# Waits by VectorE's counted work, wide products among the inverse's small ones, alternating score heads and earlier loads of the plain pair, in one layer of a hybrid trunk

## The chip, the cores and the metric

The kernel runs on one core of one Trainium2 chip. The metric is the device time of one execution in microseconds. Before the change it is 2060.8 us, the median of three runs (2058.53 to 2061.56).

## The reference

One layer on x of 1024 tokens x 1024 channels, f32: a half-weighted SwiGLU block (ffn1, width 2816), four token mixers in parallel with an output product, a second SwiGLU block (ffn2) and a final norm.

```python
def swiglu_ffn(x, w_in, w_out):
    gate, up = jnp.split(x @ w_in, 2, axis=-1)
    return (jax.nn.silu(gate) * up) @ w_out
...
    y = jnp.concatenate([y_pool, y_hgrn, y_rwkv, y_gla], axis=-1).astype(u.dtype)
    return y @ w_out
...
        x = x + 0.5 * swiglu_ffn(rms_norm(x, norm_ffn1[l]), ffn1_w_in[l], ffn1_w_out[l])
        x = x + token_mixer(rms_norm(x, norm_mix[l]), w_in[l], w_out[l], ...)
        x = x + 0.5 * swiglu_ffn(rms_norm(x, norm_ffn2[l]), ffn2_w_in[l], ffn2_w_out[l])
    return rms_norm(x, norm_final)
```

Three of the mixers carry a state along the tokens: HGRN2 and GLA are chunked gated linear attention, and RWKV7 is the recurrence

```python
        s_kk = jnp.einsum('bhvk,bhk->bhv', S, kk_t)
        S = (S * w_t[:, :, None, :] - s_kk[..., None] * (kk_t * a_t)[:, :, None, :]
             + v_t[..., :, None] * k_t[:, :, None, :])
        return S, jnp.einsum('bhvk,bhk->bhv', S, r_t)
```

The fourth is a moving average over 2 to 16 tokens. Each mixer has 256 of the 1024 channels (four heads of 64).

## The kernel before

**Precision and products.** A wide f32 product is done as three products of 128x128 by 128x512 in float32r, from a high part (`whi`, `xs`) and a low part (`wlo`, the second half of `xs`): ScalarE casts the high part, VectorE subtracts it for the low part (`wload`, lines 145 and 146, for weights; `split`, lines 177 to 181, for activations). These are the dense products here. All PE instructions go through `te.matmul` (line 89) or `te.transpose` (line 96).

**Stages.** ffn1_in, ffn1_out, the mixers (`weave`), w_out, ffn2_in, ffn2_out and the final norm. The two FFN output stages work on pairs of 128-row tiles with seven products in place of eight (`out_seven`, lines 622 to 675); one pair, PLAIN, is left for the end and done plainly: in ffn1_out its four h tiles and four weights are loaded and split after `out_seven`, then 16 output tiles follow, each of six products, whose VectorE part adds to x (line 747) and splits the sum for the mixers (line 181).

**The weave.** The mixers are generators ("threads") that do a few instructions and yield the time after which their next step may run. RWKV is one thread: four units (two pairs of heads for each half of 512 tokens) one after another. A unit fetches its inputs, prepares them on ScalarE and VectorE (lines 1206 to 1280), forms the scores (lines 1285 to 1294), inverts 64x64 triangles (`inverse`, lines 1411 to 1490: out by DMA, 28 operations on GpSimd, back by DMA, then six steps of 32 or 16 small products on PE with copies between), runs eight chunks of three steps, and starts its group norm, which stores y. GLA and HGRN2 are another thread (`gates`, lines 1491 to 1600). Two threads `rstd_steps` (lines 219 to 235) form the norm of each half. The dense stream is one generator too: the projections `w_in` of half 0 and half 1, for half 0 w_out's products (`wout_early`, line 1723), which need all of that half's y, and corner products of ffn2_in. After the weave, `w_out` does the products of half 1, which need y of the fourth RWKV unit last (ORDER, line 1707), and ffn2_in follows.

**What sets the order.** `weave` (line 882) keeps a clock `te.clk`, to which each PE instruction adds a modelled time. It takes the thread with the earliest ready time that has come, and otherwise three dense products. A yielded number of `LAT` (line 34) is added to the clock for the thread's next ready time. When the dense stream has nothing to give, the clock jumps to the next ready time. The order of PE's instructions that comes out is fixed in the program; the other engines' order follows the priorities that the steps get. The clock that the planner keeps is a model and is not measured on the chip.

Of the kernel before, what the change touches and what calls it, by code (L numbers as in the profile page):

```python
# [16 lines left out]
P = 128  # L17
# [18 lines left out]
           pool=10.0, decay=2.9, rstd=3.0, rstd1=7.0, consts=14.4, rs0=2.8, rs1=4.2)  # L36
# [32 lines left out]
class PE:  # L69
# [15 lines left out]
    def matmul(self, out, lhsT, rhs, **kw):  # L85
        n = 1
        for d in out.shape[1:]:
            n *= d
        return self._add(self.nc.tensor.matmul(out, lhsT=lhsT, rhs=rhs, **kw),  # L89
                         n * 0.42e-3 if rhs.dtype == F32R else max(n * 1.68e-3, 0.04))  # L90

    def transpose(self, out, src, ident):
        n = 1
        for d in out.shape[1:]:
            n *= d
        return self._add(self.nc.tensor.transpose(out, src, ident), max(n * 0.85e-3, 0.03))

# [6 lines left out]
class Trunk:  # L104
    def __init__(self, tc, ctx, A, out):
        self.tc, self.nc, self.A, self.out = tc, tc.nc, A, out
# [11 lines left out]
        make_identity(nc, self.ident)  # L118
# [486 lines left out]
    def out_seven(self, wk, w_out, slot, tmp, blocks, early, acc, after=None):  # L605
# [36 lines left out]
        for i, (b0, nb) in enumerate(blocks):  # L642
# [5 lines left out]
            for q in range(4):  # L648
# [28 lines left out]
                for m, w in zip(self.ORDER7, weights(raw, nb)):  # L677
# [29 lines left out]
                    if last and q == 3 and after is not None:  # L707
                        after(m)
                raw = nraw
            hs = nhs  # L710

    def ffn1_out(self, wk, w_out):
# [17 lines left out]
        def h_tile(f, h):  # L730
# [3 lines left out]

        self.out_seven(wk, w_out, slot, lambda: wk.tile([P, H], F32, name="tmp"),
                       ((9, 2), (1, 2), (3, 2), (5, 2), (7, 2)), (8, 8, 8, 8, 0), acc)
        f0 = 2 * PLAIN
        hs = [[h_tile(f, h) for h in range(2)] for f in (f0, f0 + 1)]
        w = [self.wload([(wo[:, f0:f0 + 2, n * P:(n + 2) * P], 0, None)], 2, 256, 1) for n in range(0, KT, 2)]
# [10 lines left out]
    def ffn2_out(self, wk, w_out):  # L750
# [54 lines left out]
        self.out_seven(wk, w_out, slot, tmp, ((9, 2), (1, 2), (3, 2), (5, 2), (7, 2)), (12, 12, 12, 12, 0), load_acc,  # L805
                       after)
        gf = wk.tile([P, D], F32, name="wrawb", bufs=2)
        nc.scalar.dma_start(gf, self.A["norm_final"].broadcast_to([P, D]))
        self.gf = gf

        def h_tile(f, h):
            t = tmp()
            nc.sync.dma_start(t, self.hd[f, h])
            return self.split(t)

        hp = [[h_tile(f, h) for h in range(2)] for f in (f0, f0 + 1)]
# [65 lines left out]
    def weave(self):  # L882

        te = self.te
        te.on, te.last, te.clk = True, None, 0.0
        consts = self.mix_consts()
        next(consts)
        self.threads = [Thread(self.rstd_steps(0), LAT["rs0"]), Thread(self.rstd_steps(1), LAT["rs1"]), Thread(self.ysplit()), Thread(consts, LAT["consts"]), Thread(self.rwkv()), Thread(self.gates())]
        dense = self.dense_stream()
# [12 lines left out]
    def step(self, t):  # L902
        te, tc = self.te, self.tc
        p = tc.cur_priority
        tc.cur_priority = p - URGENT
        r = next(t.gen, self)
        tc.cur_priority += URGENT
# [304 lines left out]
    def rwkv_unit(self, pr, h):  # L1212
# [72 lines left out]
        for c2 in range(4):  # L1285
            ps = self.px.tile([P, 4, P], F32, name="px")
            hd = c2 // 2
            hs = slice(hd * 64, hd * 64 + 64)
            for i in range(4):
                c = 4 * (c2 % 2) + i  # L1290
                te.matmul(ps[:, i], lhsT=bk[hs, c].rearrange("p x t -> p (x t)"), rhs=rK[hs, c].rearrange("p x t -> p (x t)"), start=True, stop=True)
            ss = slice(4 * c2, 4 * c2 + 4)
            nc.vector.tensor_tensor(Ak[:, ss], ps[:, :, 64:128], mask(64), op=ALU.mult)
            nc.vector.tensor_tensor(Ar[:, ss], ps[:, :, 0:64], mask(0), op=ALU.mult)
            if c2 in (1, 2):
                yield LAT["score"]
# [116 lines left out]
    def inverse(self, Ak):  # L1413
# [30 lines left out]
        for b in range(2):  # L1444
# [3 lines left out]
            for s in range(16):  # L1448
                te.transpose(pv[:, s], XT[bs, s, bs], self.ident[bs, bs])
# [4 lines left out]
        for b in range(2):  # L1454
            bs, b2 = slice(b * 32, b * 32 + 16), slice(b * 32, b * 32 + 32)
            for s in range(16):
                te.matmul(pv[b2, s], lhsT=XT[bs, s, b2], rhs=Xn[bs, s], start=True, stop=True)
# [4 lines left out]
        for b in range(2):  # L1462
            bs, b2 = slice(b * 32, b * 32 + 16), slice(b * 32, b * 32 + 32)
            for s in range(16):
                te.matmul(pv[bs, s], lhsT=Y[b2, s], rhs=XT[b2, s, b * 32 + 16:b * 32 + 32],
                                 start=True, stop=True)
# [8 lines left out]
        for s in range(16):  # L1475
            te.transpose(ps[0:32, s], XT[0:32, s, 0:32], self.ident[0:32, 0:32])
# [3 lines left out]
        for s in range(16):  # L1480
            te.matmul(ps[32:64, s], lhsT=XT[0:32, s, 32:64], rhs=Xn[:, s], start=True, stop=True)
# [3 lines left out]
        for s in range(16):  # L1485
            te.matmul(ps[0:32, s], lhsT=Y[32:64, s], rhs=XT[32:64, s, 32:64], start=True, stop=True)
# [366 lines left out]
```

## Time and profile before

| what | value |
|---|---|
| median of three runs | 2060.8 us (2058.53 to 2061.56) |
| the profiled execution | 2059.14 us |
| its span in the trace | 2057.3 us |
| mean granted TensorE clock | 0.983 |
| DMA | 348.60 MB, 169 GB/s |

A row of the timeline has the start, the length and the engine of one instruction or of several alike in a row (x4), then its line, operation, output<-inputs and shapes; in brackets the idle time before it on its engine and what ended that. An f32 product counts as two records, a dense product as one. A row of the busy times by stretch has the stretch, its length, the busy time of each engine with its instructions, and then the granted clock, the share of DMA and GB/s. The names: `mm`, `pg`, `px`, `pq`, `py`, `po` are banks of PSUM, `xs` split activations, `gr` and `t` tiles of RWKV, `sbd` its state, `gin`, `bdt` and `PT` tiles of GLA and HGRN2.

### The profile page before, as it was taken

What the parts mean: (1) busy time and instruction counts of PE and PEld (TensorE: products, weight loads), DVE (VectorE), ACT (ScalarE), POOL (GpSimd) and SP (SyncE); (2) the same over time, 40 slices, a digit from 0 to 9 for tenths busy, and PEclk for the clock granted to TensorE, in tenths of its full rate; (3) what the DMA queues carried; (4) which work ended last, traced back from release to release, by engine and by line L of the source; (5) the groups of instructions that cost most, each with busy time, mean ns of one, the idle gap of its engine ahead of it and who ended that gap; (6) DMA issues with size and microseconds to landing.
All of it is one profiled execution on the core that took longest, in us unless ns stands there. A gap on an engine that the chain in (4) does not pass through costs nothing. (4 is left out here: it accounts for less than half of the span.)

```text
span 2057.3 us, 29356 instructions
## 1 busy us (share of the span) xinstructions
PE 1979.4 (96%) x10424; PEld 1594.1 (77%) x10424; DVE 1541.1 (75%) x2575; ACT 964.2 (47%) x1801; POOL 442.0 (21%) x449
## 2 busy tenths in 40 slices
PE   7899999999999899989999999999999999999995
PEld 5688888887887678778778787787888887778884
DVE  5868878768878856486576676676978898777786
ACT  7435444544443655343464543444544444444444
POOL 0011110003446602002020010100111222134464
PEclk9999999999999999999999999999999999999998
DMA  8336554457653453333443244655445666786622
GB/s 275 114 93 205 200 189 161 157 186 280 253 203 138 156 159 108 91 92 97 145 147 106 83 140 134 207 172 160 139 162 187 202 211 215 242 289 254 246 89 91
DMA packets 304402, 348.60 MB, mean 169 GB/s; under 512 B 28160, under 2 KB 230240, under 8 KB 304256
## 3 DMA queue, kind: packets, MB, share of 16 engines
q1 hardware_dynamic: 301152, 339.14, 49.8%
q0 software_dynamic: 1664, 4.95, 0.7%
q10 hardware_dynamic: 1440, 2.65, 0.4%
q8 instruction: 82, 1.34, 0.3%
q14 instruction: 64, 0.52, 0.1%
HBM read 234.22 MB, written 112.46 MB: 169 GB/s over the span
## 5 line engine op out<-in xcount | busy, mean ns | idle before, releaser
L89 PE MATMUL mm<-xs,whi 128*128 128x512 f32 x1568 | 521.0, 413 | 10.3 <-ACT xs L177 3.9
L89 PEld LDWEIGHTS mm<-xs,whi 128*128 128x128 f32 x1568 | 287.4, 192 | 81.5 <-issue 8.5
L89 PE MATMUL mm<-xs,wlo 128*128 128x512 f32 x784 | 315.4, 402 | 12.1 <-DVE wlo L146 9.7
L145 ACT CAST whi<-wraw 128x512 fp32r<-128x512 f32 (+1 forms) x192 | 118.1, 620 | 171.7 <-PE mm L89 121.1
L300 ACT CAST whi<-wsum 128x512 fp32r<-128x512 f32 x176 | 108.3, 620 | 179.2 <-PE pq L89 49.4
L89 PEld LDWEIGHTS mm<-xs,wlo 128*128 128x128 f32 x784 | 150.6, 192 | 50.4 <-DVE wlo L146 12.1
L89 PE MATMUL pq<-xs,whi 128*128 128x512 f32 x576 | 181.0, 394 | 2.3 <-ACT xs L177 1.8
L146 DVE TENSOR_TENSOR wlo<-wraw,whi 128x512 fp32r<-128x512 f32 (+1 forms) x192 | 134.3, 707 | 63.2 <-ACT whi L145 51.1
L89 PE MATMUL pg<-xs,whi 128*128 128x512 f32 x560 | 176.9, 395 | 4.7 <-DVE hx L559 2.7
L89 PE MATMUL px<-xs,whi 128*128 128x512 f32 x560 | 175.2, 393 | 1.2 <-DVE xs L178 1.2
L301 DVE TENSOR_TENSOR wlo<-wsum,whi 128x512 fp32r<-128x512 f32 x176 | 121.5, 697 | 28.2 <-ACT whi L300 27.9
L89 PE MATMUL pq<-xe,whi 128*128 128x512 f32 x448 | 139.2, 392 | 0.0
L89 PEld LDWEIGHTS pq<-xs,whi 128*128 128x128 f32 x576 | 108.5, 189 | 27.2 <-ACT xs L177 2.7
L89 PEld LDWEIGHTS pg<-xs,whi 128*128 128x128 f32 x560 | 105.0, 189 | 29.5 <-issue 3.1
L89 PEld LDWEIGHTS px<-xs,whi 128*128 128x128 f32 x560 | 105.2, 188 | 25.9 <-DVE xs L178 2.3
L89 PE MATMUL pq<-xs,wlo 128*128 128x512 f32 x288 | 114.2, 396 | 3.8 <-DVE wlo L301 3.8
L340 POOL TENSOR_TENSOR tmp<-tmp 128x512 f32<-128x512 f32 x22 | 33.1, 1503 | 374.0 <-ACT tmp L330 310.6
L89 PE MATMUL pg<-xs,wlo 128*128 128x512 f32 x280 | 110.3, 394 | 0.0
L89 PE MATMUL px<-xs,wlo 128*128 128x512 f32 x280 | 109.9, 392 | 0.0
L89 PEld LDWEIGHTS pq<-xe,whi 128*128 128x128 f32 x448 | 84.3, 188 | 18.7
L622 ACT CAST whi<-wsum 128x512 fp32r<-128x512 f32 x80 | 49.7, 621 | 95.1 <-PE px L89 25.5
L340 POOL TENSOR_TENSOR gr<-gr 128x512 f32<-128x512 f32 x18 | 36.6, 2031 | 256.7 <-ACT gr L330 198.0
(460 smaller groups left out, 4319.9 us busy)
## 6 DMA issues: line engine op xcount, KB each, us to landing
hs<-hx SPq DMA_DIRECT2D x126, 512.0 KB, 3.4
xs<-hs SPq DMA_DIRECT2D x90, 512.0 KB, 6.5
wraw<-in_ffn_w_in SPq DMA_DIRECT2D x68, 512.0 KB, 4.1
wraw<-in_w_in SPq DMA_DIRECT2D x52, 512.0 KB, 4.1
wrawb<-in_ffn_w_in SPq DMA_DIRECT2D x44, 512.0 KB, 4.6
wraw<-in_ffn_w_out SPq DMA_DIRECT2D x42, 512.0 KB, 3.6
xe<-hs SPq DMA_DIRECT2D x36, 512.0 KB, 7.4
wraw<-in_w_out SPq DMA_DIRECT2D x16, 512.0 KB, 4.1
```

The lines of the kernel that those rows point to most:

```text
L89: return self._add(self.nc.tensor.matmul(out, lhsT=lhsT, rhs=rhs, **kw), n * 0.42e-3 if rhs.dtype == F32R else max(n * 1.68e-3, 0.04))
L145: nc.scalar.copy(hi[:, :n], raw[:, sl])
L146: nc.vector.tensor_tensor(lo[:, :n], raw[:, sl], hi[:, :n].bitcast(F32), op=ALU.subtract)
L300: nc.scalar.copy(hi[:, :H], a)
L301: nc.vector.tensor_tensor(lo[:, :H], a, hi[:, :H].bitcast(F32), op=ALU.subtract)
L340: nc.gpsimd.tensor_tensor(kept[5], kept[5], kept[7], op=ALU.add)
L622: nc.scalar.copy(v(hi), src)
```

## The change

It changes the order of the work and some of the tiles, and leaves the instructions on PE, VectorE and SP as many as they were (ScalarE loads a table twice more). Six edits:

- `Counted` stands around VectorE and adds up a modelled time of what the program gives it: 0.1 us and 1.15 ns for each element of a row. `backlog` compares the sum with the planner's clock, and `step` adds what VectorE is behind (`ahead`) to the ready time that a step yields.
- The planner counts 0.45 in place of 0.42 ns for a column of a dense product, and other latencies for the norms (`rstd`, `rs0`, `rs1`).
- The steps of the inverse yield "pause" after every eight small products, and `step` puts one dense step (three products) there.
- The scores fill two banks at once; products of the two heads, which lie in rows 0 to 63 and 64 to 127, alternate.
- `out_seven` calls `late(q)` four times in its last block. In ffn1_out it loads and splits one h tile and one weight of the plain pair each time; the weights lie in tiles `hx` and `xe` in place of `whi` and `wlo`.
- In ffn2_out `late` loads and splits the plain pair's h tiles, and the final norm's gain the first time.

```diff
-           pool=10.0, decay=2.9, rstd=3.0, rstd1=7.0, consts=14.4, rs0=2.8, rs1=4.2)
+           pool=10.0, decay=2.9, rstd=1.5, rstd1=7.0, consts=14.4, rs0=4.0, rs1=20.0)
...
-                         n * 0.42e-3 if rhs.dtype == F32R else max(n * 1.68e-3, 0.04))
+                         n * 0.45e-3 if rhs.dtype == F32R else max(n * 1.68e-3, 0.04))
...
+class Counted:
+    def __init__(self, eng):
+        self.eng, self.us = eng, 0.0
+    def __getattr__(self, name):
+        f = getattr(self.eng, name)
+        def call(out, *a, **kw):
+            n = 1
+            for d in out.shape[1:]:
+                n *= d
+            self.us += 0.1 + n * (2.2e-3 if name in ("copy_predicated", "tensor_tensor_scan") else 1.15e-3)
+            return f(out, *a, **kw)
+        return call
...
                     if last and q == 3 and after is not None:
                         after(m)
+                if last:
+                    late(q)
                 raw = nraw
...
+        f0 = 2 * PLAIN
+        hs, w = [[], []], []
+        def late(q):
+            hs[q // 2].append(h_tile(f0 + q // 2, q % 2))
+            raw = wk.tile([P, H], F32, name="tmp")
+            nc.sync.dma_start(raw.rearrange("p (f c) -> p f c", c=256), wo[:, f0:f0 + 2, 2 * q * P:(2 * q + 2) * P])
+            if q < 3:
+                t = wk.tile([P, 2 * H], F32R, name="hx", bufs=3)
+            else:
+                t = wk.tile([P, 2 * H], F32R, name="xe", bufs=6)
+            hi, lo = self.split(raw, t=t)
+            w.append([(hi[:, f * 256:f * 256 + 256], lo[:, f * 256:f * 256 + 256]) for f in range(2)])
-        hs = [[h_tile(f, h) for h in range(2)] for f in (f0, f0 + 1)]
-        w = [self.wload([(wo[:, f0:f0 + 2, n * P:(n + 2) * P], 0, None)], 2, 256, 1) for n in range(0, KT, 2)]
...
+    def backlog(self):
+        v = self.nc.vector
+        self.dve = max(self.dve, self.te.clk) + v.us - self.seen
+        self.seen = v.us
+        return self.dve - self.te.clk
     def step(self, t):
         te, tc = self.te, self.tc
+        ahead = max(0.0, self.dve - te.clk)
+        while True:
+            p = tc.cur_priority
+            tc.cur_priority = p - URGENT
+            r = next(t.gen, self)
+            tc.cur_priority += URGENT
+            if r != "pause":
+                break
+            next(self.dense_steps, None)
...
-            t.need, t.ready = (), te.clk + r
+            t.need, t.ready = (), te.clk + r + ahead
+        self.backlog()
...
-        for c2 in range(4):
-            ps = self.px.tile([P, 4, P], F32, name="px")
-            hd = c2 // 2
+        for half in range(2):
+            banks = [self.px.tile([P, 4, P], F32, name="px") for _ in range(2)]
             for i in range(4):
+                for hd, ps in enumerate(banks):
+                    hs = slice(hd * 64, hd * 64 + 64)
+                    te.matmul(ps[:, i], lhsT=bk[hs, 4 * half + i].rearrange("p x t -> p (x t)"),
+                              rhs=rK[hs, 4 * half + i].rearrange("p x t -> p (x t)"), start=True, stop=True)
...
-            if c2 in (1, 2):
-                yield LAT["score"]
+            if half == 0:
+                yield 2 * LAT["score"]
...
             for s in range(16):
+                if s == 8 or b and s == 0:
+                    yield "pause"
                 te.transpose(pv[:, s], XT[bs, s, bs], self.ident[bs, bs])
```

Three places show how the order moves. The names are those of the program; a number behind a name such as `sbd_6408` only tells buffers apart.

The first is PE's order near the end of the weave. Before, in the fourth unit's chunks (`py<-rhs`, `py<-gr`, `po<-gr`, `py<-sbd`), dense products (`whi`, `wlo`) stand between the steps:

```order
L89 MATMUL py<-sbd_6425,gr 64x128
L89 MATMUL py<-gr 64x64 x2
L89 MATMUL po<-sbd_6425,gr 64x128
L96 MATMUL pg<-ident,gin 128x128 x4
L89 MATMUL mm<-xs,whi 128x512 x2
L89 MATMUL mm<-xs,wlo 128x512
L89 MATMUL py<-rhs,gr 64x64 x2
L89 MATMUL mm<-xs,whi 128x512 x2
L89 MATMUL mm<-xs,wlo 128x512
L89 MATMUL pg<-gin,gg 64x64 x8
L89 MATMUL py<-gr 64x64 x2
L89 MATMUL po<-gr 64x64 x2
```

Of the change, the same engine at the end of the third unit and the start of the fourth (`px<-rin,w2a` is a unit's first product). Five chunks stand here in a row, the last of which is shown:

```order
L89 MATMUL py<-sbd_6408,gr 64x128
L89 MATMUL py<-gr 64x64 x2
L89 MATMUL po<-sbd_6408,gr 64x128
L89 MATMUL py<-rhs,gr 64x64 x2
L89 MATMUL py<-gr 64x64 x2
L89 MATMUL po<-gr 64x64 x2
L89 MATMUL px<-rin,w2a_6393 128x512 x2
L96 MATMUL px<-ident,rin 128x128 x4
L89 MATMUL px<-go,g_6396 128x512
L96 MATMUL px<-ident,go 128x128 x4
L89 MATMUL px<-sel,t 64x2 x8
L89 MATMUL px<-gr 128x128 x16
```

No dense product stands between these steps any more. Behind them there are 63 dense products of w_out ahead of the fourth unit's inverse, then that inverse and its eight chunks with none, and then the rest of w_out. Over the weave the runs of dense products are longer than before: 15 to 27 in a row stand 45 times in the change and 7 times before, where 102 runs are of 6.

The second is PE's order in an inverse's first step, its transposes (`px<-ident,gr`). Before:

```order
L96 MATMUL px<-ident,gr 16x16 x32
L89 MATMUL pg<-gin,gg 64x64 x8
L89 MATMUL px<-t,gr 32x16 x32
L89 MATMUL mm<-xs,whi 128x512 x2
L89 MATMUL mm<-xs,wlo 128x512
L89 MATMUL mm<-xs,whi 128x512 x2
L89 MATMUL mm<-xs,wlo 128x512
L89 MATMUL px<-gr,t 16x16 x32
```

Of the change, the same step of the same unit, the second:

```order
L96 MATMUL px<-ident,gr 16x16 x8
L89 MATMUL mm<-xs,whi 128x512 x2
L89 MATMUL mm<-xs,wlo 128x512
L96 MATMUL px<-ident,gr 16x16 x8
L89 MATMUL mm<-xs,whi 128x512 x2
L89 MATMUL mm<-xs,wlo 128x512
L96 MATMUL px<-ident,gr 16x16 x8
L89 MATMUL mm<-xs,whi 128x512 x2
L89 MATMUL mm<-xs,wlo 128x512
L96 MATMUL px<-ident,gr 16x16 x8
```

The 32 small products of a step are now four groups of eight, with three dense products behind each.

The third is VectorE's order at the end of ffn1_out, the last tiles of the plain pair (`gr` and `gg` hold x, `omu` is the mixers' first constant). Before:

```order
L747 SCALAR_TENSOR_TENSOR gg<-pg,gg 128x512
L181 SCALAR_TENSOR_TENSOR xs<-gg,vec,xs 128x512
L146 TENSOR_TENSOR wlo<-wraw,whi 128x512 x2
L181 SCALAR_TENSOR_TENSOR xs<-gg,vec,xs 128x512
L1023 TENSOR_SCALAR omu<-vec 128x8
```

Of the change, from the pair's first tiles (all VectorE's rows now have the line of `Counted`, 113); behind the last row shown here the pair's tiles follow with no wlo among them up to the constants:

```order
L113 SCALAR_TENSOR_TENSOR gr<-mm,gr 128x512
L113 SCALAR_TENSOR_TENSOR gr<-pg,gr 128x512
L113 TENSOR_TENSOR wlo<-wraw,whi 128x512
L113 SCALAR_TENSOR_TENSOR xs<-gr,vec,xs 128x512
L113 SCALAR_TENSOR_TENSOR gr<-mm,gr 128x512
```

The mixers' first low parts moved from behind the pair's sixteenth tile to before its chain.

More of the change, by code (lines that the diff above doesn't have):

```diff
@@ L96, in transpose, with __init__, __getattr__ @@
         return self._add(self.nc.tensor.transpose(out, src, ident), max(n * 0.85e-3, 0.03))
+class Counted:
[10 more added lines that the diff above has]
+        return call
+class Core:
+    def __init__(self, nc):
+        self.nc, self.vector = nc, Counted(nc.vector)
+    def __getattr__(self, name):
+        return getattr(self.nc, name)
 class Thread:
@@ L105, in __init__ @@
     def __init__(self, tc, ctx, A, out):
-        self.tc, self.nc, self.A, self.out = tc, tc.nc, A, out
+        self.tc, self.nc, self.A, self.out = tc, Core(tc.nc), A, out
         self.ctx = ctx
@@ L117, in __init__ @@
         self.ident = cp.tile([P, P], F32, name="ident")
-        make_identity(nc, self.ident)
+        make_identity(tc.nc, self.ident)
         self.ones = cp.tile([P, P], F32, name="ones")
@@ L603, in ahead, with out_seven @@
         return hs, steps()
-    def out_seven(self, wk, w_out, slot, tmp, blocks, early, acc, after=None):
+    def out_seven(self, wk, w_out, slot, tmp, blocks, early, acc, late, after=None):
         nc = self.nc
@@ L804, in ffn2_out, with late @@
         f0 = 2 * PLAIN
-        self.out_seven(wk, w_out, slot, tmp, ((9, 2), (1, 2), (3, 2), (5, 2), (7, 2)), (12, 12, 12, 12, 0), load_acc,
[L806 to L816, printed above, removed]
+        hp = [[], []]
+        def late(q):
+            if q == 0:
+                gf = self.gf = wk.tile([P, D], F32, name="wrawb", bufs=2)
+                nc.scalar.dma_start(gf, self.A["norm_final"].broadcast_to([P, D]))
+            t = tmp()
+            nc.sync.dma_start(t, self.hd[f0 + q // 2, q % 2])
+            hp[q // 2].append(self.split(t))
+        self.out_seven(wk, w_out, slot, tmp, ((9, 2), (1, 2), (3, 2), (5, 2), (7, 2)), (12, 12, 12, 12, 0), load_acc,
+                       late, after)
         for c in range(2):
@@ L885, in weave @@
         te.on, te.last, te.clk = True, None, 0.0
+        self.dve, self.seen = 0.0, self.nc.vector.us
         consts = self.mix_consts()
@@ L888, in weave @@
         self.threads = [Thread(self.rstd_steps(0), LAT["rs0"]), Thread(self.rstd_steps(1), LAT["rs1"]), Thread(self.ysplit()), Thread(consts, LAT["consts"]), Thread(self.rwkv()), Thread(self.gates())]
-        dense = self.dense_stream()
+        dense = self.dense_steps = self.dense_stream()
         while True:
@@ L912, in step @@
         else:
-            t.need, t.ready = (), te.clk + r
+            t.need, t.ready = (), te.clk + r + ahead
+        self.backlog()
     def spawn(self, gen, us):
@@ L1284, in rwkv_unit @@
         mask = lambda o: self.rmask[:, o:o + 64].unsqueeze(1).broadcast_to([P, 4, 64])
-        for c2 in range(4):
-            ps = self.px.tile([P, 4, P], F32, name="px")
-            hd = c2 // 2
-            hs = slice(hd * 64, hd * 64 + 64)
+        for half in range(2):
+            banks = [self.px.tile([P, 4, P], F32, name="px") for _ in range(2)]
             for i in range(4):
[L1290 to L1294, printed above, removed]
-            if c2 in (1, 2):
-                yield LAT["score"]
+                for hd, ps in enumerate(banks):
+                    hs = slice(hd * 64, hd * 64 + 64)
+                    te.matmul(ps[:, i], lhsT=bk[hs, 4 * half + i].rearrange("p x t -> p (x t)"),
+                              rhs=rK[hs, 4 * half + i].rearrange("p x t -> p (x t)"), start=True, stop=True)
+            for hd, ps in enumerate(banks):
+                ss = slice(8 * hd + 4 * half, 8 * hd + 4 * half + 4)
+                nc.vector.tensor_tensor(Ak[:, ss], ps[:, :, 64:128], mask(64), op=ALU.mult)
+                nc.vector.tensor_tensor(Ar[:, ss], ps[:, :, 0:64], mask(0), op=ALU.mult)
+            if half == 0:
+                yield 2 * LAT["score"]
         AkL = Ak[0:64].rearrange("p (x c) t -> p x c t", x=2)
@@ L1456, in inverse @@
             for s in range(16):
+                if s == 8 or b and s == 0:
+                    yield "pause"
                 te.matmul(pv[b2, s], lhsT=XT[bs, s, b2], rhs=Xn[bs, s], start=True, stop=True)
@@ L1464, in inverse @@
             for s in range(16):
+                if s == 8 or b and s == 0:
+                    yield "pause"
                 te.matmul(pv[bs, s], lhsT=Y[b2, s], rhs=XT[b2, s, b * 32 + 16:b * 32 + 32],
@@ L1475, in inverse @@
         for s in range(16):
+            if s == 8:
+                yield "pause"
             te.transpose(ps[0:32, s], XT[0:32, s, 0:32], self.ident[0:32, 0:32])
@@ L1480, in inverse @@
         for s in range(16):
+            if s == 8:
+                yield "pause"
             te.matmul(ps[32:64, s], lhsT=XT[0:32, s, 32:64], rhs=Xn[:, s], start=True, stop=True)
@@ L1485, in inverse @@
         for s in range(16):
+            if s == 8:
+                yield "pause"
             te.matmul(ps[0:32, s], lhsT=Y[32:64, s], rhs=XT[32:64, s, 32:64], start=True, stop=True)
```

7 lines of the change are left out of this document (1 added, 6 removed).

## The prediction

> **What bounds the kernel now.** The page's first part and its table of slices come first, then the busy times by stage (columns: stretch, its length, busy us of PE, PEld, DVE, ACT and POOL with instruction counts, granted TensorE clock, DMA share, GB/s).
>
> ```profile
> span 2057.3 us, 29356 instructions
> PE 1979.4 (96%) x10424; PEld 1594.1 (77%) x10424; DVE 1541.1 (75%) x2575; ACT 964.2 (47%) x1801; POOL 442.0 (21%) x449
> ...
> 24.00:663.40 639.40, 626.93 (x2713) 507.76 (x2711) 506.75 (x776) 298.36 (x531) 141.52 (x96) 0.99 0.53 184
> 663.40:702.60 39.20, 27.87 (x107) 20.30 (x107) 38.02 (x49) 25.81 (x43) 27.35 (x21) 0.91 0.47 170
> 702.60:1312.00 609.40, 596.30 (x4433) 477.01 (x4432) 394.89 (x829) 287.47 (x593) 76.99 (x182) 0.97 0.42 123
> 1312.00:1420.00 108.00, 105.89 (x469) 85.36 (x469) 73.90 (x119) 44.18 (x74) 6.06 (x8) 1.00 0.57 176
> ...
> 951.70:961.90 10.20, 10.20 (x113) 8.80 (x111) 0.63 (x3) 1.77 (x5) 0.00 (x0) 0.50 0.12 38
> ```
>
> PE is the bound: busy 96% of the span. So time can be won only where PE stands idle or runs at a lower clock, and it is lost wherever the new order leaves PE with nothing to do. The stage before the mixers (663.4 to 702.6) has 39.20 - 27.87 = 11.3 us idle and 0.09 x 39.2 = 3.5 us of clock. The weave of the mixers (702.6 to 1312.0) has 13.1 us idle and 0.03 x 609.4 = 18.3 us of clock. That is all the change can win there, 46 us, and 31 of them in the weave. The last row is one piece of that clock: PE busy for all of 10.2 us, with the inverse's small products, at half clock.
>
> **The change part by part.** First, the plain pair at the end of ffn1_out.
>
> ```profile
> 663.21 0.39 PE L89 MATMUL pq<-xs,wlo 128*128 128x512 f32 x1
> 666.40 0.50 PE L89 MATMUL mm<-xs,whi 128*128 128x512 f32 x1 [2.81 <-ACT xs L177]
> ...
> 699.44 0.79 PE L89 MATMUL mm<-xs,wlo 128*128 128x512 f32 x1 [7.00 <-DVE wlo L146]
> ```
> ```profile
> 696.90 0.68 DVE L747 SCALAR_TENSOR_TENSOR gg<-pg,gg 128x512 f32<-128x512 f32 x1
> 697.50 1.27 DVE L181 SCALAR_TENSOR_TENSOR xs<-gg,vec,xs 128x512 fp32r<-128x512 f32 x1
> 698.70 2.36 DVE L146 TENSOR_TENSOR wlo<-wraw,whi 128x512 fp32r<-128x512 f32 x2
> ```
>
> PE waits 2.81 us for the pair's loads and later 7.00 us for wlo, the mixers' first weights, whose splits stand behind the pair's last tiles on DVE. After the change the loads and splits stand in the block before, and the first wlo stands ahead of the pair's tiles. The first wait goes; most of the second goes. What is late next is DVE's own chain, 0.6 + 1.2 us for each of 16 tiles (rows of 696.90 to 698.70), against six products of 0.23 us, 1.4 us. I take -10 us, with bounds -12 (both waits and a little clock) and -5 (the chain hands part of it back).
>
> The eight splits that this part adds to the last block of the seven lie beside the block's own DVE work:
>
> ```profile
> 643.90:663.10 19.20, 19.20 (x85) 15.61 (x84) 19.03 (x24) 7.31 (x13) 15.25 (x11) 1.00 0.11 37
> ...
> 652.28 0.68 DVE L623 TENSOR_TENSOR wlo<-wraw,whi 128x512 fp32r<-128x512 f32 x1
> 652.88 1.78 DVE L623 TENSOR_TENSOR wlo<-wsum,whi 128x512 fp32r<-128x512 f32 x1
> ```
>
> In the block's second half DVE is busy 19.03 of 19.20 us, and one split took 0.68 us or, beside POOL, 1.78. Eight of them are 5.4 to 14.2 us, with little room; I cost them at nothing because PE had two stalls' worth of slack right behind (that is in the -5 bound), and keep the rest as a rival. ffn2_out gets the same edit; its end has waits of 1.03 and 0.92 us:
>
> ```profile
> 2008.26 0.66 PE L794 MATMUL px<-ident,gr 128*128 128x128 f32 x4 [1.03 <-ACT xe L796]
> ...
> 2013.64 0.33 PE L794 MATMUL px<-ident,gr 128*128 128x128 f32 x1 [0.92 <-DVE gr L675]
> ```
>
> I take -2.5 us for them, the two and a little of the turns behind; bounds 0 and -3.4.
>
> Second, the scores. Two products that sit in different row halves overlap; a unit's 16 score products now alternate.
>
> ```profile
> 735.34 1.13 PE L89 MATMUL px<-rin,w2a 64*128 64x512 f32 x4
> 749.50 1.98 PE L89 MATMUL px<-raw,glaw 16*128 16x512 f32 x4
> 905.78 2.05 PE L89 MATMUL px<-gr 64*128 64x128 f32 x16
> ```
>
> Two products in different halves took 1.13 us (two records each), two in the same rows 1.98. Eight score products take 2.05 us, a unit's sixteen 4.1, so alternation saves up to 0.43 of that: 1.75 us a unit, three covered units. I take -5; bounds 0 and -7.
>
> Third, the waits for the counted backlog and the later ready times. They put more dense products before each step of a thread, so that PE no longer meets a step whose DVE work is behind, as here:
>
> ```profile
> 888.42 2.04 PE L89 MATMUL pg<-bdt,gin 128*128 128x128 f32 x8 [6.38 <-DVE PT L1547]
> ```
>
> Of the weave's 31 us of idle time and clock I take two thirds, -21; bounds -8 and -29. The pauses inside the inverse split each run of small products by three dense ones. A turn costs: 6 dense products between two small steps took 985.45 - 983.88 = 1.57 us (rows below), while 21 in one run took 1344.43 - 1339.55 = 4.88, 0.232 each, so 6 would be 1.39. At 0.18 to 0.25 us each, 36 covered pauses are +7 us; bounds 0 (the turn was there anyway) and +14.
>
> Fourth, and against all this: dense products are a fixed stock. Where more stand before each step, the stock is used up earlier. The rows of the order show it: after the third unit's third chunk no dense product stands until the fourth unit's end, but for 63 of w_out's (three banks) ahead of its inverse. So five chunks and one whole unit of RWKV run bare, and w_out's other products, which wait for that unit's y, stand behind them. The price is the wall time of that serial chain less what its steps cost PE under cover. From rows of units that ran under cover:
>
> ```profile
> 978.73 0.44 PE L89 MATMUL py<-rhs,gr 64*64 64x64 f32 x4
> 979.57 0.27 DVE L1348 TENSOR_TENSOR gr<-py,nn 64x128 f32<-64x128 f32 x1
> ...
> 981.09 0.60 DVE L1361 SCALAR_TENSOR_TENSOR sbd<-py,wc,Sw 64x64 f32<-64x64 f32 x2 [0.52 <-PE py L89]
> ...
> 983.67 0.26 ACT L1337 COPY rhs<-py 64x128 f32<-64x128 f32 x1 [1.56 <-PE py L89]
> 983.88 0.73 PE L89 MATMUL mm<-xs,whi 128*128 128x512 f32 x2
> ...
> 985.45 0.44 PE L89 MATMUL py<-rhs,gr 64*64 64x64 f32 x4
> ...
> 1167.06 0.69 DVE L1387 TENSOR_REDUCE gmu<-go 128x8 f32<-128x512 f32 x1 [0.26 <-ACT go L1385]
> ...
> 1183.33 0.75 DVE L1269 SCALAR_TENSOR_TENSOR t<-rin,vec,t 128x512 f32<-128x512 f32 x1
> ...
> 1201.23 1.20 DVE L1298 TENSOR_TENSOR gr<-gr,nn 64x1024 f32<-64x1024 f32 x1
> ```
> ```profile
> 1202.46 0.32 SPq L1420 DMA_DIRECT2D ld<-gr  x1
> ...
> 1223.47 1.79 SPq L1438 DMA_DIRECT2D gr<-xd  x4
> ```
> ```profile
> 800.55 0.87 PE L96 MATMUL px<-ident,gr 16*16 16x16 f32 x32
> ...
> 815.91 1.19 PE L89 MATMUL px<-gr,t 32*32 32x32 f32 x32
> ```
> ```profile
> 1305.42 0.58 DVE L1361 SCALAR_TENSOR_TENSOR sbd<-py,wc,Sw 64x64 f32<-64x64 f32 x2 [0.26 <-PE py L89]
> ...
> 1326.40 0.32 SPq L1102 DMA_DIRECT2D rin<-pd_y  x1
> ```
> ```profile
> 1339.55 0.62 PE L89 MATMUL mm<-xs,whi 128*128 128x512 f32 x2
> ...
> 1344.43 0.62 PE L89 MATMUL pg<-xs,whi 128*128 128x512 f32 x2
> ```
>
> - A chunk is a ring: copy to rhs, product, DVE's gr, product, DVE's sbd, product. Covered it took 985.45 - 978.73 = 6.72 us with 18 dense products (4.2), so 2.6 us of PE. Bare, the ring's own parts (three DVE or ACT steps of 0.26 to 0.60, products of 0.3 to 0.44, and the turns between engines) are an estimated 3.2 us at full clock and 4.0 at half; I take 3.6. Thirteen chunks: 47 (42 to 52).
> - From the chunks' end to the scores' last mask under cover: 1202.43 - 1167.06 = 35.4 us, of which DVE's own chain to 1184.08 is 17.0. Bare I take 21 (18 to 26).
> - The inverse's round trip by DMA and POOL: first issue at 1202.46, last at 1225.26, and about 3 us to land: 26 (24 to 30).
> - Its six product steps: 16.6 us under cover; bare 14 (12 to 20, the latter at half clock).
> - Group norm, y written, read back and split: 1326.72 - 1305.42 = 21.3 to the read's issue, under cover; bare, to the split's end, 18 (16 to 21).
>
> The wall is 126 us, 112 to 149. Under cover the same steps cost PE 13 x 2.6 = 34, 10 for the inverse's products and turns, 7 for preparation and scores, and the 63 dense products 14.6: 65 us. So the tail costs +61, bounds +47 and +84. A smaller place of this kind is at the first half's end, where the dense stream waits for that half's y with few products left: by the same chain, 0 to +15; I take +6.
>
> [...]
>
> **The sum.** -10 - 2.5 - 5 - 21 + 7 + 6 + 61 = +35.5 us on the profiled execution's 2059.1 (span 2057.3 and 1.8 around it); that execution lies 1.7 below the median of the runs, 2060.8. So 2096.
>
> **The rivals.**
> - *The tail is short and the stalls pay for it: faster.* One chain decides, the bare one. If it ran at the shortest of the bounds or less (chunks 2.6, the wall 98), it would cost +33; with the other terms at their good ends (-12 - 3.4 - 7 - 29 = -51) the sum is -18: 2043. The point from which it decides is a wall of 65 + 25.5 = 90 us with my middle terms, 116 with the good ends. For it speaks that DVE and ACT are free of the dense stream's splits there; against it that four DMA legs and 28 POOL steps cannot be shortened.
> - *Half clock through the whole tail.* The row of 951.70 speaks for it: small products alone got 0.50. Wall 149, +84: 2119.
> - *The last block becomes DVE's.* Eight splits at 0.68 to 1.78 us against 0.2 us free in the second half: +8 more, 2104.
> - *The change does not do what it says*, because the planner's clock only shifts: 2061. The order of the products speaks against it, since the dense runs in it are longer and end earlier.
>
> **How the numbers follow.** A measurement of this kernel can tell about 0.2%, 4 us, from no change. Chances: the forecast 0.62, half clock throughout 0.14, DVE's block 0.08, faster 0.11, no effect 0.05. The forecast's bounds on the tail alone give 2082 to 2119; the good ends of the other terms reach to 2064. The range is 2064 to 2120: it leaves out the faster rival and the upper half of the half-clock one. Slower 0.84, same 0.05, faster 0.11.
>
> **What would show it.** Right: about 125 us before w_out's main part in which PE is busy under two thirds, DVE low, and PE's waits are for DVE sbd and gr, ACT rhs and the inverse's DMA; no 7 us wait for wlo; no 6 us wait for PT; score records in pairs. Wrong: if PE's share in that stretch stays above 80%, or the stretch is under 90 us, the tail was overrated, and the time comes out at or below 2061.

## The result, and the profile after

| | before | after |
|---|---|---|
| median | 2061.12 us (2058.53 to 2061.56, 4 runs) | 2158.51 us (2151.18 to 2161.33, 4 runs) |
| ratio | | 1.047, 95% interval 1.044 to 1.050: slower |
| span of the profiled execution | 2057.3 us | 2154.1 us |
| mean granted TensorE clock | 0.983 | 0.954 |

The direction was forecast, the size was not: +97 us against +35, and the time lies above the range. (Of the experiments below, one execution of the earlier loads alone took 6298.1 us; its ratio leaves that one out.)

The first part of the page after the change:

```profile
span 2154.1 us, 29360 instructions
PE 2018.8 (94%) x10424; PEld 1616.2 (75%) x10424; DVE 1544.9 (72%) x2575; ACT 969.6 (45%) x1803; POOL 443.5 (21%) x449
```

The instructions on PE and VectorE are as many as before, so all that is added is time in which PE is idle or slow. Busy times by stretch, of the kernel before:

```profile
640.00:740.00 100.00, 88.17 (x426) 71.31 (x425) 73.89 (x106) 51.33 (x90) 58.30 (x59) 0.97 0.44 143
740.00:1420.00 680.00, 665.29 (x4684) 530.26 (x4683) 454.56 (x917) 315.17 (x636) 70.11 (x161) 0.97 0.43 129
```

and of the kernel after:

```profile
640.00:740.00 100.00, 88.38 (x419) 70.59 (x418) 71.82 (x103) 49.89 (x87) 58.62 (x59) 0.97 0.41 129
740.00:1180.00 440.00, 427.09 (x2919) 344.47 (x2919) 282.54 (x581) 207.12 (x417) 36.15 (x86) 0.97 0.41 120
1180.00:1220.00 40.00, 23.27 (x120) 16.60 (x119) 29.22 (x57) 14.21 (x28) 2.00 (x1) 0.77 0.36 106
1220.00:1347.00 127.00, 125.62 (x844) 97.51 (x843) 71.28 (x135) 46.42 (x85) 13.24 (x32) 0.97 0.43 130
1347.00:1477.00 130.00, 89.86 (x660) 63.92 (x656) 49.60 (x110) 34.88 (x78) 19.09 (x42) 0.61 0.22 68
1477.00:1510.00 33.00, 33.00 (x134) 26.51 (x135) 21.63 (x35) 15.83 (x28) 0.00 (x0) 0.93 0.50 152
```

A stretch loses its length less PE's busy time at the granted clock. The 680 us of before lose 680 - 665.29 x 0.97 = 35 us. The same work after takes 770 us and loses 26 + 22 + 5 + 75 + 2 = 130. So the bare tail (1347 to 1477) lost 75 us and the thin place at the first half's end (1180 to 1220) 22. The covered rest of the weave lost 33, as much as all of it did before. The clock has two digits, so such a sum is good to some 3 us for each 600.

Rows of PE in the tail: a chunk at full clock, the fourth unit's first product, its inverse's first transposes and its first chunk, a chunk at half clock, and the unit's end:

```profile
1348.78 0.43 PE L89 MATMUL py<-sbd,gr 128*64 128x128 f32 x2
...
1351.94 0.43 PE L89 MATMUL py<-sbd,gr 128*64 128x128 f32 x2 [0.55 <-DVE sbd L113]
...
1367.23 2.08 PE L89 MATMUL px<-rin,w2a 64*128 64x512 f32 x4
...
1412.45 0.55 PE L96 MATMUL px<-ident,gr 16*16 16x16 f32 x16 [3.98 <-DMA gr<-xd]
...
1426.47 0.69 PE L89 MATMUL py<-sbd,gr 128*64 128x128 f32 x2
...
1443.14 0.69 PE L89 MATMUL py<-sbd,gr 128*64 128x128 f32 x2 [0.28 <-DVE sbd L113]
...
1447.30 0.69 PE L89 MATMUL py<-sbd,gr 128*64 128x128 f32 x2 [0.28 <-DVE sbd L113]
...
1459.46 2.08 PE L89 MATMUL px<-go,g 128*128 128x512 f32 x2
1469.53 1.09 PE L96 MATMUL px<-ident,go 128*128 128x128 f32 x4 [7.99 <-DVE go L113]
1476.78 1.52 PE L89 MATMUL mm<-xs,whi 128*128 128x512 f32 x2 [6.16 <-ACT xs L206]
```

A bare chunk takes 3.16 us at full clock (1348.78 to 1351.94, granted 1.00) and 4.16 at half (1443.14 to 1447.30, granted 0.50). From the last chunk to w_out's first product PE waits for the group norm on VectorE and for y's way through memory, 18 us.

The long waits of PE elsewhere, at the mixers' start and (last row) in the thin place; the row between them is the first RWKV unit's first product:

```profile
704.88 2.08 PE L89 MATMUL px<-ident,rstok 128*128 128x128 f32 x8 [6.66 <-POOL rstok L256]
...
736.88 1.13 PE L89 MATMUL px<-rin,w2a 64*128 64x512 f32 x4
...
1199.24 2.08 PE L89 MATMUL px<-st,pw 128*128 128x512 f32 x2 [12.57 <-DVE st L113]
```

The 7.00 us for wlo are gone, but 6.66 us for rstok stand in their place, and the first RWKV unit starts at 736.88 against 735.34 before. In the covered part (740 to 1180) the longest waits are for ScalarE's Sb (total us, times, longest):

```profile
PE pg L89 <- ACT Sb L1644: 6.7, 2, 5.2
```

### The profile page after: what moved, and what is told of

The parts are those of the page before. It is cut to its first block, busy times and chain, and to the rows that moved or that the text cites. A ratio compares the mean times of both kernels' runs of the same rounds, so it can differ in the third digit from the quotient of the medians.

```text
span 2154.1 us, 29360 instructions
## 1 busy us (share of the span) xinstructions
PE 2018.8 (94%) x10424; PEld 1616.2 (75%) x10424; DVE 1544.9 (72%) x2575; ACT 969.6 (45%) x1803; POOL 443.5 (21%) x449
## 5 line engine op out<-in xcount | busy, mean ns | idle before, releaser
L89 PE MATMUL mm<-xs,whi 128*128 128x512 f32 x1536 | 510.8, 413 | 11.2 <-ACT xs L206 6.6
L113 DVE TENSOR_TENSOR wlo<-wraw,whi 128x512 fp32r<-128x512 f32 (+2 forms) x308 | 216.0, 705 | 135.8 <-ACT whi L174 95.8
L89 PE MATMUL mm<-xs,wlo 128*128 128x512 f32 x768 | 309.2, 403 | 4.1 <-DVE wlo L113 4.1
L113 DVE TENSOR_TENSOR wlo<-wsum,whi 128x512 fp32r<-128x512 f32 x256 | 190.0, 747 | 49.5 <-ACT whi L329 28.3
L89 PE MATMUL pg<-xs,whi 128*128 128x512 f32 x528 | 169.3, 401 | 3.7 <-DVE hx L113 2.7
L89 PEld LDWEIGHTS pg<-xs,whi 128*128 128x128 f32 x528 | 100.0, 192 | 27.3 <-issue 3.1
L89 PE MATMUL pg<-xs,wlo 128*128 128x512 f32 x264 | 104.9, 398 | 0.0
```

The lines of the kernel that those rows point to most:

```text
L113: return f(out, *a, **kw)
```

## The experiments

Each ratio is to the kernel before on the same chip.

**Without the counted wait (e1).**

```diff
-            t.need, t.ready = (), te.clk + r + ahead
+            t.need, t.ready = (), te.clk + r
```

> The whole change, but a step's ready time is te.clk + r again, without what VectorE is counted behind. Theory A (the added wait alone spends the dense stock early: bare tail and thin place, 94 of the 97 us lost): 2050 to 2067 us, no stretch in which RWKV runs without dense products, mean granted clock at or above 0.98. Theory B (all edits together slow the threads, the wait is one of several): above 2090 us.

Measured: 2091.47 us against 2066.87, ratio 1.0116 (1.0089 to 1.0143). The tail is gone, 73 of the 97 us with it, and the clock is 0.982. But the time is not back, and it lies in theory B's range: A named the cause of the tail rightly and missed that the other edits cost 24 us.

**The counted wait alone (e2)**, in the kernel before.

> The kernel before with the counted wait alone. Theory A: 2145 to 2170 us, with a tail of 120 to 135 us at about 0.6 of the clock. Theory B: below 2100 us.

Measured: 2149.95 us against 2066.87, 1.0401 (1.0371 to 1.0431), +83 us, as theory A said. Its weave up to the tail, and the tail:

```profile
742.00:1348.00 606.00, 575.92 (x3928) 467.09 (x3924) 386.72 (x781) 270.52 (x537) 49.03 (x119) 0.95 0.41 123
1348.00:1475.00 127.00, 91.18 (x617) 66.04 (x616) 48.93 (x105) 35.30 (x77) 19.55 (x42) 0.57 0.20 61
```

The tail's 127 us lose 127 - 91.18 x 0.57 = 75, as in the full change. Up to it 606 - 575.92 x 0.95 = 59 us are lost, against 26 + 22 + 5 = 53 there: the wait alone takes no stalls away either. The wait and all other edits, +83 and +24, give 107 where the whole change has 97.

**RWKV later by a constant (e9)**, in the kernel before, with nothing counted: 1.4 us for each step of that thread.

```diff
-            t.need, t.ready = (), te.clk + r
+            t.need, t.ready = (), te.clk + r + (1.4 if t.gen.__name__ == "rwkv" else 0.0)
```

> The kernel before, where each step of the RWKV thread alone is ready 1.4 us later in the planner's clock (the mean that the counted wait adds to it) and nothing is counted. Theory A (the bare tail comes from RWKV's serial chain being served later than the dense stock lasts, whatever the reason): 2140 to 2165 us, with a tail of 110 to 130 us. Theory E (the harm is in which steps the counted wait delays): below 2110 us.

Measured: 2132.89 against 2063.83, 1.0332 (1.0305 to 1.0358), +69, with a tail of 110 us:

```profile
1350.00:1460.00 110.00, 76.79 (x555) 57.73 (x556) 44.77 (x93) 31.28 (x68) 18.63 (x42) 0.61 0.25 77
```

That is below A's range by 7 us, and by far nearer to A than to E: what makes the tail is that the serial chain is served later than the dense stock lasts, and not what the wait counts. The thin place is another matter. In the full change PE has no dense product for 30.9 us there (from 1183.74) and in e2 for 30.0 (from 1175.41); in e9 such a gap lasts at most 8.0 us ahead of its tail. So RWKV served later does not make the thin place by itself, and which thread does was not separated.

**Useless dense products in the tail (e8)** of the full change, three wherever the planner had nothing to give.

```diff
-                    te.clk = max(te.clk, min(t.ready for t in self.threads if all(k in self.stored for k in t.need)))
+                    to = min(t.ready for t in self.threads if all(k in self.stored for k in t.need))
+                    if len(self.ys) == KT and te.clk < to:
+                        hi, lo = self.ys[0]
+                        ps = self.bank()
+                        for i in range(3):
+                            te.matmul(ps, lhsT=hi[:, 0:P], rhs=hi, start=i == 0, stop=i == 2)
+                    te.clk = max(te.clk, to)
```

> The whole change, and in the bare tail three idle dense products (of data that nobody reads) wherever the planner has nothing to give. Theory C (half clock is a price of its own in the tail, 15 to 20 us, and products without use keep the clock up): 2135 to 2148 us, clock in the tail above 0.9. Theory D (the ring of VectorE, ScalarE and DMA sets the wall; the products only stand in its way): 2155 to 2185 us whatever the clock.

Measured: 2177.14 against 2066.73, 1.0539 (1.0503 to 1.0576). The time lies in theory D's range and is slower than the full change. But the clock was not kept up throughout, so C's own condition was not met, and half clock's price in the tail isn't measured by this run. Two stretches behind the inverse's round trip, and one ahead of it:

```profile
1414.60:1441.90 27.30, 24.64 (x278) 18.10 (x279) 0.69 (x2) 3.54 (x8) 0.00 (x0) 0.50 0.06 13
1441.90:1460.00 18.10, 18.10 (x89) 10.94 (x87) 2.55 (x9) 2.85 (x9) 0.00 (x0) 0.72 0.00 1
1340.00:1370.00 30.00, 30.00 (x176) 19.73 (x174) 11.21 (x26) 7.79 (x20) 0.00 (x0) 1.00 0.25 83
```

```profile
1440.01 1.65 PE L89 MATMUL pg<-xs 128*128 128x512 f32 x3
```

In the first stretch PE was busy for nine tenths of the time and granted 0.50, and its three useless products (the row, of PE's timeline) took 1.65 us. In the last stretch, ahead of the round trip, chunks with the same useless products ran at 1.00.

**The scores' alternation alone (e4).**

> The kernel before with the alternating heads of the scores alone. Theory A (rows 0 to 63 and 64 to 127 overlap, 1.75 us a unit in four covered units): 2053 to 2057 us. Theory B (the masks on VectorE or the dense order take it back): 2059 to 2063 us. The score records should start in pairs a few ns apart.

Measured: 2075.85 against 2066.87, 1.0045 (1.0029 to 1.0062): slower by half a per cent, above the ranges of both theories. The group of the score products, before and with the edit:

```profile
L89 PE MATMUL px<-gr 64*128 64x128 f32 x128 | 17.6, 283 | 0.0
```
```profile
L89 PE MATMUL px<-gr 64*128 64x128 f32 x128 | 11.2, 288 | 0.7 <-DVE gr L113 0.4 <-DVE n L113 0.3
```

PE's time on them falls by 6.4 us at much the same length of a record (288 ns for 283), so the records overlap more. In the trace of the full change, which has the same edit, 41 of the 64 pairs of such records start 6 to 14 ns apart, as A said they should; before, no two start less than 111 ns apart. The gain is there and is lost elsewhere. The waits of PE in its weave (us in total, times, longest):

```profile
PE pg L89 <- DVE gin L113: 7.0, 2, 6.0
PE px L89 <- DMA go<-pd_xg: 6.4, 1, 6.4
PE mm L89 <- ACT gat L1222: 2.8, 1, 2.8
```

The 6.4 us for go are new; for gin the longest was 1.2 us before.

**The pauses alone (e5), and the planner's numbers alone (e6)**. The edit shown is that of e6; e5 is the change's part of that name.

```diff
-           pool=10.0, decay=2.9, rstd=3.0, rstd1=7.0, consts=14.4, rs0=2.8, rs1=4.2)
+           pool=10.0, decay=2.9, rstd=1.5, rstd1=7.0, consts=14.4, rs0=4.0, rs1=20.0)
...
-                         n * 0.42e-3 if rhs.dtype == F32R else max(n * 1.68e-3, 0.04))
+                         n * 0.45e-3 if rhs.dtype == F32R else max(n * 1.68e-3, 0.04))
```

> The kernel before with the pauses in the inverse alone (36 to 48 more turns between small and dense products). Theory A (a turn costs 0.18 to 0.25 us, and the half clock in the inverse goes): +7 for the turns, -7 for the clock, 2056 to 2066 us, with no half-clock stretch beside an inverse. Theory B (any edit that shifts the planner's order throws the few long waits of the weave elsewhere, and more of them appear): 2066 to 2085 us, with waits over 2 us in places where before has none.

> The kernel before with the new planner numbers alone (0.45 ns for a dense column, norm latencies 1.5, 4.0 and 20.0). Theory A (they move little, and the counted wait does the harm): 2056 to 2066 us. Theory B (any shift of the order brings new waits, and rstd at 1.5 puts the norm's second half ahead of its time): 2068 to 2085 us, with a wait of about 6 us for rstok at the start of the mixers.

Measured: 2120.66 against 2066.73, 1.0270 (1.0222 to 1.0317), and 2105.84, 1.0211 (1.0170 to 1.0253). Both lie above B's own ranges. The sign that B named for e6, some 6 us for rstok at the mixers' start, isn't there: PE waits 7.0 us for wlo, as before. The weave of e5 loses 12.25 us at one place; SP's queue, then PE:

```profile
1236.84 0.32 SPq L1142 DMA_DIRECT2D pd_xg<-st  x1
1240.59 0.32 SPq L1148 DMA_DIRECT2D go<-pd_xg  x1
```
```profile
1243.34 2.07 PE L89 MATMUL px<-go,g 128*128 128x512 f32 x2 [12.25 <-DMA go<-pd_xg]
```

The product that PE stands on needs a tile that was stored 6.5 us before and fetched 2.75 us before. The store had waited for VectorE's and ScalarE's last work on that tile (1234.64 to 1235.38 and 1236.19 to 1236.82), work of the dense stream, which the steps of the threads overtake there. The planner's clock knows neither queue. Waits are not all of it. The weave of e5:

```profile
742.40:1480.00 737.60, 689.70 (x4679) 535.13 (x4677) 454.93 (x917) 321.47 (x639) 72.05 (x161) 0.96 0.40 118
```

PE is idle for 47.9 us (14.7 before), and its busy time at its clock is 689.70 x 0.96 = 662 us, against 665.29 x 0.97 = 645: some 17 us more for the same products in more turns.

**One planner number changed by 2% (e12)**, in the kernel before.

```diff
-                         n * 0.42e-3 if rhs.dtype == F32R else max(n * 1.68e-3, 0.04))
+                         n * 0.43e-3 if rhs.dtype == F32R else max(n * 1.68e-3, 0.04))
```

> The kernel before with one planner number changed by 2% (0.43 in place of 0.42 ns for a dense column), which moves some 120 runs of PE's order. Theory B (the order of before is one that suits the chip, and any other brings more and longer waits): 2072 to 2105 us. Theory A (small shifts are neutral): 2056 to 2068 us.

Measured: 2094.02 against 2063.83, 1.0139 (1.0107 to 1.0171), +30 us. Its weave:

```profile
741.00:1454.00 713.00, 683.72 (x4686) 544.84 (x4684) 455.39 (x916) 317.14 (x638) 71.35 (x161) 0.95 0.41 123
```

713 us against 680. The idle time is 29.3 us, against 14.7 before, and the clock 0.95 against 0.97: a shift that means nothing doubles the idle time. B holds.

**PE's order kept, the other engines' changed (e15)**: the threads' steps at the priority of the dense stream (in the kernel before). The priority orders the work of every engine but PE, so VectorE's order is not the only one that moves.

```diff
-CORNERS, MORE, URGENT = 4, 4, 80
+CORNERS, MORE, URGENT = 4, 4, 0
```

> The kernel before with the threads' steps at the same priority as the dense stream: PE's order stays word for word, VectorE's changes. Theory G (the weave's waits come from where VectorE's work of a thread stands against that of the dense stream; with PE's order fixed another order there makes other waits): more than 10 us away from 2061, with other waits over 2 us. Theory H (PE's order alone decides): 2055 to 2067 us.

Measured: 2087.25 against 2066.23, 1.0095 (1.0071 to 1.0119), +21 us. Its longest waits in the weave:

```profile
PE pg L89 <- DVE PT L1547: 6.8, 1, 6.8
PE pg L89 <- DVE gin L1542: 4.9, 3, 2.7
PE px L89 <- DVE n L1278: 3.0, 1, 3.0
PE px L96 <- ACT go L1405: 2.7, 1, 2.7
```

The first stood before too (6.4 us, for the same tile); those for n and go are new. So H falls: the waits hang on the order of the other engines as well as on PE's. That it is VectorE's alone, as G has it, is not shown; the wait for go was for ScalarE.

**A quarter of the wait**, in the full change (e10) and with the earlier loads alone (e11).

```diff
-            t.need, t.ready = (), te.clk + r + ahead
+            t.need, t.ready = (), te.clk + r + 0.25 * ahead
```

> The whole change with a quarter of the counted wait. The order has no bare tail. Theory A (the full wait keeps the other edits' new waits down and pays for it with the tail; a part of it keeps some of the first without the second): 2066 to 2090 us, between the change without the wait (2091) and the kernel before. Theory B (each order throws the waits anew, unrelated to the wait's size): 2090 to 2120 us.

> The kernel before with the earlier loads and a quarter of the counted wait, none of the other edits. Theory A: 2050 to 2066 us, with fewer waits for VectorE in the weave than before. Theory B: 2070 to 2110 us.

Measured: 2107.27 and 2106.05 against 2063.83, 1.0210 (1.0184 to 1.0236) and 1.0194 (1.0158 to 1.0230). Neither has the bare tail, and both are worse than the same edits with no wait at all (1.0116 in e1, 0.9984 in e3 below). A smaller wait buys nothing: theory A's second half falls, and B holds.

**The earlier loads alone (e3)**, in both output stages.

> The kernel before with the earlier loads and splits of the plain pair alone (both output stages). Theory A (VectorE's chain over the pair's 16 tiles, 28 us before and after, sets the end of ffn1_out, and the loads were never what ended last): 2057 to 2064 us. Theory B (the prediction's -10 - 2.5 is there but was lost to the new norm latencies of the full change): 2046 to 2053 us.

Measured: 2063.00 against 2066.87, 0.9984 (0.9966 to 1.0003): no difference that can be told, as A says.

**The sums of squares left out (e7)** at the end of ffn1_out, beside the earlier loads.

```diff
             nc.scalar.activation(t, x, AF.Square)
-            nc.gpsimd.tensor_tensor(self.sq[h], self.sq[h], t, op=ALU.add)
```

> The earlier loads alone, and GpSimd's sums of squares left out (the norm of the mixers then comes from one tile's squares). Theory A (VectorE's chain sets the pair's end, and GpSimd beside it stretches its second step from 0.74 to 1.2 us): the 16 tiles take 22 to 24 us instead of 28, and the time falls by 4 to 8 us against the earlier loads alone, 2053 to 2059 on the scale of 2061. Theory B (PE or the loads set it): 27 to 28 us as before and no gain.

Measured: 2049.16 against 2066.73, 0.9926 (0.9901 to 0.9951). VectorE's split of one tile in the full change, with GpSimd's addition beside it, and in this kernel:

```profile
687.44 1.57 DVE L113 SCALAR_TENSOR_TENSOR xs<-gr,vec,xs 128x512 fp32r<-128x512 f32 x1
...
697.25 2.26 DVE L113 SCALAR_TENSOR_TENSOR xs<-gg,vec,xs 128x512 fp32r<-128x512 f32 x2
```
```profile
688.04 0.75 DVE L113 SCALAR_TENSOR_TENSOR xs<-gr,vec,xs 128x512 fp32r<-128x512 f32 x1
...
692.76 0.75 DVE L113 SCALAR_TENSOR_TENSOR xs<-gg,vec,xs 128x512 fp32r<-128x512 f32 x1 [0.19 <-ACT xs L209]
```

The pair's chain takes 21.1 us in place of 28.3 and ends at 693.5 in place of 699.5, and the wait behind it is gone. Both the chain and the time (2046 us on the scale of 2061) gained more than A said. The sums themselves, for which the norm waits, are gone here too; the next two runs keep them.

**The sums of squares on PE**, with the earlier loads (e13) and without (e14): a tile of squares times ones, accumulated over the eight tiles of a half, in place of GpSimd's additions.

```diff
-        self.sumsq_add(wk, h, self.x[k, h])
...
+        nc.scalar.activation(t, self.x[k, h], AF.Square)
...
+                self.te.matmul(self.ss_ps, lhsT=self.onesr, rhs=t, start=kk == 0, stop=kk == KT - 1)
...
+            nc.scalar.activation(self.sq[h], self.ss_ps, AF.Identity, scale=1.0 / P)
```

> The earlier loads alone, and the sums of squares at the end of ffn1_out on PE (one product of a 128x512 tile of squares with ones for each of the 16 tiles, in place of GpSimd's 14 additions). Theory A (GpSimd beside VectorE sets the pair's end, and the loads' gain lies behind that): the chain takes 20 to 22 us, PE spends 3.7 us more, the wait of 7 us at the start of the mixers is gone, 2051 to 2058 us on the scale of 2061. Theory F (the mixers' start waits for the norm's sums whatever their engine): 2059 to 2064.

> The sums of squares on PE, without the earlier loads. Theory A in its strong form (GpSimd's share was all, the loads nothing): as with the loads, 2051 to 2058 us. If the loads matter once VectorE is free: 2058 to 2064 us, with the waits for the loads (2.8 us) and for wlo still there.

Measured: 2056.06 and 2054.48 against 2066.23, 0.9961 (0.9944 to 0.9978) and 0.9938 (0.9914 to 0.9963). Both beat the kernel before and the kernel after. The two intervals overlap, so the earlier loads add nothing that can be told. On the scale of 2061 that is 2053 and 2048 us, at or below A's range, so F falls. The end of ffn1_out to the weave in e14, and the first RWKV unit's first product:

```profile
640.00:732.00 92.00, 87.95 (x431) 72.67 (x430) 64.42 (x102) 50.34 (x89) 35.99 (x45) 0.98 0.48 153
...
727.75 1.13 PE L89 MATMUL px<-rin,w2a 64*128 64x512 f32 x4
```

92 us against 100, with the 16 added products in it; the unit starts 7.6 us earlier than before. VectorE's splits took 0.74 or 0.75 us in e14, and the wait for wlo is gone, while 3.5 us for the pair's loads are still there. In e13's profile the chain took 26.6 us, not the 20 to 22 of A, with VectorE now waiting for PE's products (eight waits, 3.6 us in all), and the unit starts only 1.8 us earlier; where the rest of its gain lies was not separated.

## Why the prediction was too low, point by point

1. **What bounds the kernel: right.** PE's work stayed; the loss is idle time and clock.
2. **The tail, "+61, bounds +47 and +84": right in mechanism, and mis-sized within its bounds.** The wall was 130 us where 126 was worked out, and it loses 75 us. The chunks were 3.16 us at full clock and 4.16 at half, where 3.2 and 4.0 were estimated, 51 us in all for 47. Preparation, scores and the inverse's round trip, from 1367.23 to 1412.45, were 45 us for 47, the inverse's products 14 for 14, the end 18 for 18. So the wall, with its clock of 0.61, accounts for 4 of the 14 us that are missing; the rival with half clock throughout had 149. The other 10 are in what was taken off: the same work was booked at 65 us of PE under cover, and what PE did in the tail is worth 89.86 x 0.61 = 55. That PE would be busy under two thirds was nearly so: 69%, much of it at half clock. e1, e2 and e9 show that the later service of the RWKV thread makes the tail. That small products alone got 0.50 is not what the row of 951.70 shows, for nine dense products stand among them there; in the tail small products alone got 1.00 from 1348.78 to 1355.0 and 0.50 from 1426.47 to 1459.46. The 3 us booked for the landing of the inverse's last loads are shown by no run: in the trace of before these landed in 1.7 to 2.0 us, so that the round trip booked at 26 us took 24.1, from 1202.46 to 1226.60.
3. **The thin place, "0 to +15; I take +6": mis-sized.** It lost 22 us: 16.7 of PE idle, 12.57 of them in one wait for VectorE's st, and the rest by a clock of 0.77. As in the tail the dense stream has nothing to give, and e1 shows that the counted wait makes it; but it isn't the RWKV chain alone, since e9 has next to none of it.
4. **"Of the weave's 31 us of idle time and clock I take two thirds, -21": this is the step that failed.** The covered parts lost as much as before, 33 us against 35. The 6.4 us wait for PT that it named is gone, and others, 6.7 us for Sb first, stand in its place. The premise was that a longer distance between steps takes waits away. In e2, the wait alone, they are not fewer. The runs show that the waits go with the whole order, PE's against that of the other engines, and that other orders wait elsewhere. Every other order of the weave that was tried is slower, whatever its edit was for: 0.5% for the scores, 2.7% for the pauses, 2.1% for the planner's numbers, 1.4% for a shift of 2%, 1.0% with PE's order untouched. The costs do not add: scores, pauses and numbers are 9 + 54 + 39 = 102 us one by one, and all edits without the wait 24.
5. **The pauses, "+7": wrong in size by itself** (+54 alone). In e5 PE's own work grew by some 17 us, more than twice the +7 for turns; most of the rest is idle time, for the reason of point 4.
6. **The scores, "-5": the mechanism is right, the sum is not.** PE saves 6.4 us on them, and the kernel is 9 us slower, by point 4.
7. **The plain pair, "-10, bounds -12 and -5": wrong.** The loads' wait was not what ended last: VectorE's chain over the pair's 16 tiles takes 27.6 us before and 27.7 after, without the wlo that stand in it (29.9 and 28.3 with them), since GpSimd's additions beside it stretch each split from 0.75 to 1.2 or 1.6 us. The prediction had the chain as "what is late next" and then let it hand back half. With GpSimd out of the way the first RWKV unit starts 10.1 us earlier in e7, and 7.6 in e14, which has no early loads.
8. **ffn2_out, "-2.5": not there.** From the norm's product at the weave's end to the end of the span it is 2057.3 - 1421.73 = 635.6 us before and 2154.1 - 1514.41 = 639.7 after. The 4 us come with the counted wait: e2, which has the wait and not this edit, has 2148.2 - 1508.50 = 639.7, and e1, which has the edit and not the wait, 2090.6 - 1454.60 = 636.0. How the wait makes them was not separated. The two waits at the end, 1.03 and 0.92 us before, are 1.5 and 0.3 after. The rows are of before, after, e2 and e1:

```profile
1421.73 1.16 PE L89 MATMUL px<-ident,rstok 128*128 128x128 f32 x8 [1.15 <-POOL rstok L227]
```
```profile
1514.41 1.16 PE L89 MATMUL px<-ident,rstok 128*128 128x128 f32 x8 [1.18 <-POOL rstok L256]
```
```profile
1508.50 1.72 PE L89 MATMUL px<-ident,rstok 128*128 128x128 f32 x8 [1.18 <-POOL rstok L256]
```
```profile
1454.60 1.16 PE L89 MATMUL px<-ident,rstok 128*128 128x128 f32 x8 [1.16 <-POOL rstok L256]
```

So the sum of +35 was short by 62 us: 21 for stalls that stayed, 16 at the thin place, 14 in the tail, 11 at the pair, and 6 behind the weave; these are 68. Against them PE's work in the weave fell by some 6 us at its clock (645 to 640), where pauses and scores were booked at +2.

That each order tried has its own waits is shown. Why the order of before has so few is not: it may have been picked among many.

## What to carry to other kernels

When a planner's order is changed, count first how long the filler lasts: a serial chain that is served later by a little at each step runs bare at the end, and its price is its whole wall time less what PE's work in it is worth (here 130 - 55 = 75 us). Do not book the stalls of a schedule as a gain of a better rule before its noise is known; change one number by 2% first and see how far the time moves (here 1.4%), since any edit of the order is read against that. Where VectorE's chain ends last, look for what GpSimd does beside it before moving loads (here a split of 0.75 us took 1.2 to 1.6).

## What the runs showed of the hardware that was not expected

- The clock stayed at half through long work: in e8, after a wait of 18.09 us for the inverse's gr, PE was busy for 24.64 of 27.30 us at 0.50 and then for 18.10 of 18.10 at 0.72, with useless dense products among the small ones. So PE's records show some 27 us of mostly busy time without the full clock. Why is open; small f32 products stand between the dense ones, but so they do in the stretch at 1.00, ahead of that wait.
- VectorE's split takes 0.74 or 0.75 us alone and 1.2 to 1.6 us beside GpSimd's additions. In the change the additions run from 674.38 to 700.63, and the split at 673.01, ahead of them, took 0.74 us. In e7, without the additions, all 16 took 0.74 or 0.75 us. How GpSimd's work stretches VectorE's was not shown.
